# One-core encoder layer: transfers in another order, one more spinning matmul call, rows of x requested five steps ahead, the bias table built without TensorE, the last step by token halves

## The chip, the cores and the metric

The kernel runs on one core of a Trainium2 chip. The metric is the device time of one execution in microseconds. The engines are named as in the profile: PE multiplies matrices (PEld are its weight loads), DVE and ACT work on vectors, POOL does nothing of weight here, and SP only issues transfers (rows marked SPq).

## The reference, cut to what matters

```
xn = rms_norm(x, norm_g)                        # x: 256 tokens x 4096
h  = xn @ w_in                                  # 4096 x 14336
c_val, c_glu, c_gate, q, k, v, a_gate = split(h)
conv_out = silu(layer_norm(conv31(c_val * sigmoid(c_glu)))) * silu(c_gate)
attn_out = dilated_attention(rms(q), rms(k), v, rel_bias) * silu(a_gate)
y  = x + concat(conv_out, attn_out) @ w_out     # 4096 x 4096
```

All is float32. The relative bias is a table of 32 buckets by 16 heads, looked up by the bucket of the distance, plus the logarithm of how many of the three dilation patterns hold that distance.

## The kernel before, in words

The products are done in 18 groups of 1024 output columns: 14 groups of `w_in` columns (4 for the convolution, 8 for attention, 2 for the gate), then 4 of `w_out`. A group is 32 steps of 128 input channels; step n of the whole program (n from 0 to 575) handles channel block k = n mod 32. To keep float32 accuracy each operand is split in two parts in a shorter format: `wh` (ACT, L196) and `wl` (DVE, L197) of the weights, `xh` (ACT, L244) and `xl` (DVE, L245) of x. A step is 12 matmuls: for two column halves e and two token halves s, `xh*wh` (L621), `xl*wh` (L622) and `xh*wl` (L624).

Weights arrive as `raw` tiles, 1 MB each, one for two steps; three of them exist. The transfer of `raw(j+3)` is written right after the second split of `raw(j)` and waits for it. Splits are written three steps ahead of the products (`AHEAD = 3`). The transposed x arrives as `xT` tiles (four blocks each after the first few), and is split in the first group only and kept. In the same group the eight chunks of plain x (`x0` to `x7`, 512 KB each) are read to get the row norm: `load_x` requests a chunk, `square_x` (ACT, L237) squares it two and three steps later. From the sums `finish_rstd` makes `rstd`; as its yields are written out in the main loop, its root on ACT (L149) falls into step 29 and its end (L257) into step 30. The evacuation of the first group needs it at the end of step 31 (L575 on ACT for column half 0, L578 on DVE for half 1).

Nearly all transfers are issued by SP, strictly in program order: one whose wait is not met holds back all behind it. Every engine also takes its own instructions in program order. The bias table is made in `setup_gen`: a one-hot matrix times the table on PE (L281), a copy on ACT, and a store to `bias_dram`, from which attention reads it back much later. At the end of each `out` group, x is added to the accumulators (L563) and the result is stored (L565).

Of the kernel before, what the change touches and what calls it, by code (L numbers as in the profile page):

```python
# [11 lines left out]
F32 = mybir.dt.float32  # L12
# [20 lines left out]
DVE_STEP, ACT_STEP = 950, 1400  # L33
AHEAD = 3
RAW = 3
XN_LOAD = {2 + 3 * c: c for c in range(8)}
XN_SQUARE = {4 + 3 * c + s: (c, s) for c in range(8) for s in range(2)}
EVAC_TABLE = {"conv": AF.Sigmoid, "agv": AF.Silu, "gate": AF.Silu}
C_VAL, C_GLU, C_GATE, C_Q, C_K, C_V, C_AG = (2048 * i for i in range(7))

# [8 lines left out]
VECS = {"conv_b": 0, "ln_g": 16, "ln_b": 32, "q_g": 48, "k_g": 49}  # L49


def _bias_index():


    out = np.zeros((RB + 1, NDEL), np.float32)
    half, exact, dmax = RB // 2, RB // 4, 1024
    for m in range(NDEL):
        d = m - (S - 1)
        n = abs(d)
        if n < exact:  # L60
            b = n
        else:
            b = exact + int(
                np.float32(np.log(np.float32(n) / np.float32(exact)))
                / np.float32(math.log(dmax / exact))
                * np.float32(half - exact)
            )
            b = min(b, half - 1)
        b += half if d > 0 else 0
        out[b, m] = 1.0  # L70
        c = int(n <= 64) + int(n % 4 == 0 and n <= 256) + int(n % 16 == 0 and n <= 1024)
        out[RB, m] = math.log(c) if c else NEG
    return out


class Lane:
# [28 lines left out]
def layer_kernel(  # L105
# [4 lines left out]
    w,  # L110
    vecs,
    conv_w,
    rel_bias,
    bias_index,
    out,
):
    nc = tc.nc
# [9 lines left out]
    def t2(name):  # L127
        return sb.tile([P, 512], F32, tag="t2", bufs=6, name=name)
# [4 lines left out]
    def side(name):  # L133
        return ps.tile([P, 512], F32, tag="side", bufs=4, name=name)
# [36 lines left out]

    raw_tiles = {}

    def load_pair(j, cuts=(0, 2048)):

        g, jj = divmod(j, n_pairs)
        if g >= NG:
            return
        if groups[g][0] == "out":
            jj = (jj + n_pairs // 2) % n_pairs  # L180
        rt = sb.tile([P, 2048], F32, tag="raw", bufs=RAW, name=f"raw{j}")
        raw_tiles[j] = rt.rearrange("p (k c) -> p k c", k=2)
        for lo, hi in zip(cuts, cuts[1:]):
            nc.sync.dma_start(rt[:, lo:hi], w[g, jj, :, lo:hi])

    w_split = {}

# [76 lines left out]
    def setup_gen():  # L264
        for _ in range(8):
            yield
        nc.sync.dma_start(vec_cols, vecs)
        nc.sync.dma_start(wT.rearrange("p a b -> p (a b)"), conv_w)
        for _ in range(4):
            yield  # L270
        nc.vector.tensor_mul(gqk, col("q_g"), col("k_g"))
        yield
        rb = const.tile([RB + 1, NH], F32, name="rb")
        nc.gpsimd.memset(rb, 1.0)
        nc.sync.dma_start(rb[0:RB, :], rel_bias)
        oh = t2("oh")
        nc.sync.dma_start(oh[0 : RB + 1, :], bias_index)
        for _ in range(4):
            yield
        pb = side("pb")  # L280
        nc.tensor.matmul(pb[0:NH, :], rb, oh[0 : RB + 1, :], start=True, stop=True)  # L281
        yield
        tb = t2("tb")
        nc.scalar.copy(tb[0:NH, :], pb[0:NH, :])
        nc.sync.dma_start(bias_dram, tb[0:NH, :])
        yield

    aT, cT, mixA = {}, {}, {}
    conv_ready = {}
# [264 lines left out]

    xr_tiles = {}

    def evacuate(g, e, accs):
        kind, idx = groups[g][:2]
        rstd = state.get("rstd")
        if kind == "out":  # L560
            for s in range(2):
                t = xr_tiles[(g, e)][:, s, :]
                nc.vector.tensor_add(t, t, accs[s])  # L563
                c = groups[g][2 + e]
                nc.sync.dma_start(out[0][P * s : P * s + P, c : c + 512], t)  # L565
            return
        if kind == "conv" and e == 1:
            pair = state["sig"]
# [31 lines left out]

    accs = {}

    def products(n, e, part):

        g, k = divmod(n, KT)
# [24 lines left out]

    nc.scalar.dma_start(first_x, x_cols[:, 0 : KT + S])
    xT[0] = first_x[:, KT:]
    load_pair(0, (0, 512, 1024, 2048))
    load_xT(1, 1, nc.scalar)
    load_xT(2, 2, nc.scalar)
    load_pair(1, (0, 1024, 2048))
    load_xT(4, 4, nc.sync)
    load_pair(2)
    nc.scalar.copy(warm, ones[:, 0:1])
    spin = side("spin")  # L640
    for _ in range(6):
        nc.tensor.matmul(spin[:, :P], ones, ones, start=True, stop=True)

    split_w(0)
# [2 lines left out]
    for n in range(NG * KT):  # L647
# [19 lines left out]
        else:  # L667
# [8 lines left out]
            split_w(n + AHEAD)  # L676
            if k < KT - 1:
                products(n, 0, 1)
            else:
                products(n, 1, 0)  # L680
                products(n, 1, 1)
        if n % 4 == 0 and 8 + n < KT:
            load_xT(8 + n, 4, nc.sync)
        if n in XN_LOAD:
            load_x(XN_LOAD[n])
        if n in XN_SQUARE:
            square_x(*XN_SQUARE[n])
        if k == KT - 3 and groups[g][0] in EVAC_TABLE:
            nc.scalar.activation(warm, ones[:, 0:1], EVAC_TABLE[groups[g][0]])  # L689
        if 28 <= n <= 29:  # L690
            next(rstd_steps)
        elif n == 30:
            list(rstd_steps)
        pump()


_BIAS_INDEX = _bias_index()


def _layout(i):  # L700
# [4 lines left out]

    w_in, w_out = i["w_in"][0], i["w_out"][0]
    n_pairs = KT // 2
    w = np.empty((len(GROUPS), n_pairs, P, 2, 2, 512), np.float32)
    for g, (kind, _, *firsts) in enumerate(GROUPS):
        src = w_out if kind == "out" else w_in  # L710
# [8 lines left out]
        "w": w.reshape(len(GROUPS), n_pairs, P, 2048),  # L719
        "vecs": np.concatenate([cols(v) for v in vecs], axis=1),  # L720
        "conv_w": i["conv_w"][0].T.reshape(16, P, TAPS).transpose(1, 0, 2).reshape(P, -1),
        "rel_bias": i["rel_bias"],
        "bias_index": _BIAS_INDEX,
    }


# [27 lines left out]
```

## Time and profile before

| What | Value |
|---|---|
| Three runs | 1616.45, 1618.78 (median), 1620.45 us |
| Profiled execution, its own time | 1618.36 us |
| Its span in the profile | 1616.6 us |
| PE busy | 1605.7 us, 99% of the span, 7058 rows |
| DVE busy | 1072.2 us, 66% |
| ACT busy | 926.5 us, 57% |
| Moved by the core | 323.54 MB, mean 200 GB/s |

The profiled execution's own time is 1.76 us more than its span and 0.42 us below the median of the runs. Busy PE does not mean PE at its best: what a stretch costs is read from the starts of its matmuls.

### The profile page before, as it was taken

How to read it: one execution, taken by the hardware profiler on the slowest of the kernel's cores; microseconds unless marked ns; L12 is line 12 of the kernel's file. 1: busy time of each engine (PE TensorE's matmuls, PEld its weight loads, DVE VectorE, ACT ScalarE, POOL GpSimd, SP SyncE). 2: the span in 40 equal slices, each digit the busy share in tenths (PEclk: the TensorE clock that was granted, in tenths of full speed). 3: DMA queues.
4: the chain of work that ended last, by engine and by line, in shares of the span. 5: the costliest groups of instructions: out<-in, count | busy, mean ns of one | idle time of the engine just before them, and what ended most of it. 6: DMA issues, size and time to landing. Idle time of an engine off the chain costs nothing.

```text
span 1616.6 us, 18843 instructions
## 1 busy us (share of the span) xinstructions
PE 1605.7 (99%) x7058; PEld 1326.2 (82%) x7058; DVE 1072.2 (66%) x1440; ACT 926.5 (57%) x1415; POOL 0.3 (0%) x5
## 2 busy tenths in 40 slices
PE   8999999999999999999999999999999999999998
PEld 7878888888888888888888888888888888888887
DVE  5557888888888888678765555556466565454543
ACT  5664454545463456775778756774667973333332
POOL 0000000000000000000000000000000000000000
PEclk9999999999999999999999999999999999999999
DMA  8855555555555555555554555545555566566663
GB/s 308 326 182 189 202 185 190 199 197 194 190 201 185 202 186 194 191 180 186 205 185 176 200 188 192 192 176 197 201 194 179 194 210 228 212 222 220 214 229 104
DMA packets 52808, 323.54 MB, mean 200 GB/s; under 512 B 5819, under 2 KB 8251, under 8 KB 16108
## 3 DMA queue, kind: packets, MB, share of 16 engines
q1 hardware_dynamic: 52284, 321.79, 55.7%
q8 instruction: 55, 0.90, 0.2%
q10 hardware_dynamic: 432, 0.54, 0.1%
q14 instruction: 37, 0.30, 0.0%
HBM read 318.08 MB, written 4.23 MB: 199 GB/s over the span
## 4 chain that ended last, share of the span: by engine, by line
PE 96%; DMA 1%; ACT 1%; issue 0%; DVE 0%; SPq 0%; DVEq 0%; ACTq 0%
PE acc L621 32%; PE acc L622 31%; PE acc L624 31%; PE psc L475 1%; PE po L514 1%; DMA raw<-in_w_dram 1%; ACT wh L196 1%; DMA x<-in_x_dram 0%; ACT cT L400 0%; DMA first_x<-in_x_cols_dram 0%; DVE wl L197 0%; ACT qk L314 0%; ACT L689 0%; PE pb L281 0%; ACT conv L575 0%
## 5 line engine op out<-in xcount | busy, mean ns | idle before, releaser
L197 DVE TENSOR_TENSOR wl<-raw,wh 128x1024 fp32r<-128x1024 f32 x575 | 703.7, 1224 | 501.0 <-ACT wh L196 498.4
L196 ACT CAST wh<-raw 128x1024 fp32r<-128x1024 f32 x575 | 604.6, 1052 | 622.3 <-PE acc L622 433.4
L621 PE MATMUL acc<-wh,xh 128*128 128x512 f32 x1792 | 705.4, 394 | 5.2 <-ACT xh L244 1.8
L622 PE MATMUL acc<-wh,xl 128*128 128x512 f32 x1792 | 699.2, 390 | 0.0
L624 PE MATMUL acc<-wl,xh 128*128 128x512 f32 x1792 | 484.1, 389 | 0.0
L621 PEld LDWEIGHTS acc<-wh,xh 128*128 128x128 f32 x1792 | 337.4, 188 | 78.4 <-ACT conv L575 2.5
L622 PEld LDWEIGHTS acc<-wh,xl 128*128 128x128 f32 x1792 | 337.5, 188 | 70.2 <-DVE xl L245 0.2
L624 PEld LDWEIGHTS acc<-wl,xh 128*128 128x128 f32 x1792 | 336.3, 188 | 70.7 <-DVE wl L197 0.3
L346 DVE SCALAR_TENSOR_TENSOR cT<-conv,wT,cT 128x241 f32<-128x241 f32 (+14 forms) x480 | 201.6, 471 | 0.0
L621 PE MATMUL acc<-wh,mh 128*128 128x512 f32 x512 | 199.2, 389 | 0.0
L622 PE MATMUL acc<-wh,ml 128*128 128x512 f32 x512 | 199.2, 389 | 0.0
L624 PE MATMUL acc<-wl,mh 128*128 128x512 f32 x512 | 138.1, 389 | 0.0
L621 PEld LDWEIGHTS acc<-wh,mh 128*128 128x128 f32 x512 | 96.1, 188 | 20.0
L622 PEld LDWEIGHTS acc<-wh,ml 128*128 128x128 f32 x512 | 96.1, 188 | 20.0
L624 PEld LDWEIGHTS acc<-wl,mh 128*128 128x128 f32 x512 | 96.1, 188 | 19.9
L505 ACT COPY pr<-turn_p 32x128 f32<-32x128 f32 x256 | 75.9, 296 | 5.3 <-DVE turn_p L499 1.9
L245 DVE SCALAR_TENSOR_TENSOR xl<-xT,first_x,xh 128x256 fp32r<-128x256 f32 x31 | 14.9, 480 | 21.0 <-ACT xh L244 21.0
L314 ACT COPY qk<-turn_q 32x256 f32<-32x256 f32 x64 | 25.9, 404 | 1.2
L314 ACT COPY qk<-turn_k 32x256 f32<-32x256 f32 x64 | 25.8, 403 | 1.2 <-DVE turn_k L306 0.2
L314 ACT COPY agv<-turn_ag 32x256 f32<-32x256 f32 x64 | 25.8, 404 | 1.0
L314 ACT COPY conv<-turn_a 32x256 f32<-32x256 f32 x64 | 25.8, 403 | 1.1
L314 ACT COPY gate<-turn_g 32x256 f32<-32x256 f32 x64 | 25.9, 404 | 1.0
(126 smaller groups left out, 401.5 us busy)
## 6 DMA issues: line engine op xcount, KB each, us to landing
raw<-in_w_dram SPq DMA_DIRECT2D x286, 1024.0 KB, 4.8
x<-in_x_dram SPq DMA_DIRECT2D x8, 512.0 KB, 8.1
xr<-in_x_dram SPq DMA_DIRECT2D x8, 512.0 KB, 5.7
out_dram<-xr SPq DMA_DIRECT2D x16, 256.0 KB, 5.3
xT<-in_x_cols_dram SPq DMA_DIRECT2D x7, 512.0 KB, 7.7
T<-bias_dram SPq DMA_DIRECT2D x16, 192.0 KB, 4.9
raw<-in_w_dram SPq DMA_DIRECT2D x3, 512.0 KB, 8.9
raw<-in_w_dram SPq DMA_DIRECT2D x2, 256.0 KB, 5.2
```

The source lines that it names most:

```text
L196: nc.scalar.copy(wh, src)
L197: nc.vector.tensor_sub(wl, src, wh.bitcast(F32))
L245: nc.vector.scalar_tensor_tensor(l, src, g_cols[:, k : k + 1], h.bitcast(F32), op0=ALU.mult, op1=ALU.subtract)
L314: nc.scalar.copy(dst[32 * b : 32 * b + 32, :, :, to, :], backwards(v) if flip else v)
L346: nc.vector.scalar_tensor_tensor(c[:, t, lo:hi], a[:, t, lo + sh : hi + sh], wT[:, ch, k : k + 1], c[:, t, lo:hi], op0=ALU.mult, op1=ALU.add,)
L475: nc.tensor.matmul(psc[:, it, :], qt[hg][:, hh, P * it : P * it + P], kt[hg][:, hh, :], start=True, stop=True,)
L505: nc.scalar.copy(dst[32 * b : 32 * b + 32, :, :, 3 - a, :], backwards(blocks[32 * a : 32 * a + 32, :, :, b, :]),)
L514: nc.tensor.matmul(po[:, :S], vt[hg][:, jt, hs], pT[:, jt, :], start=jt == 0, stop=jt == 1)
L621: nc.tensor.matmul(a, hs, wp, start=k == 0, stop=False)
L622: nc.tensor.matmul(a, ls, wp, start=False, stop=False)
L624: nc.tensor.matmul(a, hs, wp, start=False, stop=k == KT - 1)
```

## The change

The first `xT` transfers move from ACT's queue to SP's, each between the pieces of `raw` beside which it is used, and `xT8` is requested before the loop. The spin loop has seven calls in place of six (each call shows as two PE rows, so 14 in place of 12). A chunk of x is requested five and six steps ahead of its two squares, in place of two and three, and the chunks follow every 2.5 steps, in place of 3. The steps of `finish_rstd` are written two to one step earlier: root in step 27, end in step 29. The bias table comes from two host-arranged rows per head that one DVE addition joins. In the last step of the program the three products of token half 0 all stand ahead of those of half 1, and half 1 is added and stored in two pieces of 256 columns, the first issued by ACT, the second by SP.

```diff
-XN_LOAD = {2 + 3 * c: c for c in range(8)}
-XN_SQUARE = {4 + 3 * c + s: (c, s) for c in range(8) for s in range(2)}
+XN_LOAD = {1 + (5 * c + 1) // 2: c for c in range(8)}
+XN_SQUARE = {n + 5 + s: (c, s) for n, c in XN_LOAD.items() for s in range(2)}
...
-    def load_pair(j, cuts=(0, 2048)):
+    def load_pair(j, cuts=(0, 2048), between=None):
...
             nc.sync.dma_start(rt[:, lo:hi], w[g, jj, :, lo:hi])
+            if between and hi == 1024:
+                between()
...
-        rb = const.tile([RB + 1, NH], F32, name="rb")
-        nc.gpsimd.memset(rb, 1.0)
-        nc.sync.dma_start(rb[0:RB, :], rel_bias)
-        oh = t2("oh")
-        nc.sync.dma_start(oh[0 : RB + 1, :], bias_index)
+        tb = t4("tb").rearrange("p a b -> p (a b)")[0:NH, :]
+        nc.sync.dma_start(tb, bias_rows)
         for _ in range(4):
             yield
-        pb = side("pb")
-        nc.tensor.matmul(pb[0:NH, :], rb, oh[0 : RB + 1, :], start=True, stop=True)
-        yield
-        tb = t2("tb")
-        nc.scalar.copy(tb[0:NH, :], pb[0:NH, :])
-        nc.sync.dma_start(bias_dram, tb[0:NH, :])
-        yield
+        nc.vector.tensor_add(tb[:, :NDEL], tb[:, :NDEL], tb[:, NDEL:])
+        nc.sync.dma_start(bias_dram, tb[:, :NDEL])
+        yield 600
...
+    def add_out(g, e, s, acc, queues=(nc.sync,)):
+        c, n = groups[g][2 + e], 512 // len(queues)
+        for i, queue in enumerate(queues):
+            t = xr_tiles[(g, e)][:, s, n * i : n * i + n]
+            nc.vector.tensor_add(t, t, acc[:, n * i : n * i + n])
+            queue.dma_start(out[0][P * s : P * s + P, c + n * i : c + n * i + n], t)
...
+    def last_products(n):
+        g, k = divmod(n, KT)
+        wh, wl = (t[:, 512:] for t in w_split[n])
+        for s in range(2):
+            a = accs[(g, 1)][s]
+            hs, ls = (t[:, P * s : P * s + P] for t in (mh[k], ml[k]))
+            nc.tensor.matmul(a, hs, wh, start=False, stop=False)
+            nc.tensor.matmul(a, ls, wh, start=False, stop=False)
+            nc.tensor.matmul(a, hs, wl, start=False, stop=True)
+            add_out(g, 1, s, a, (nc.scalar, nc.sync) if s else (nc.sync,))
...
-    load_pair(0, (0, 512, 1024, 2048))
-    load_xT(1, 1, nc.scalar)
-    load_xT(2, 2, nc.scalar)
+    load_pair(0, (0, 512, 1024, 2048), between=lambda: load_xT(1, 1, nc.sync))
+    load_xT(2, 2, nc.sync)
     load_pair(1, (0, 1024, 2048))
     load_xT(4, 4, nc.sync)
     load_pair(2)
+    load_xT(8, 4, nc.sync)
     nc.scalar.copy(warm, ones[:, 0:1])
     spin = side("spin")
-    for _ in range(6):
+    for _ in range(7):
         nc.tensor.matmul(spin[:, :P], ones, ones, start=True, stop=True)
...
-        if n % 4 == 0 and 8 + n < KT:
-            load_xT(8 + n, 4, nc.sync)
+        if n % 4 == 0 and 12 + n < KT:
+            load_xT(12 + n, 4, nc.sync)
...
-        if 28 <= n <= 29:
+        if 26 <= n <= 28:
             next(rstd_steps)
-        elif n == 30:
+        elif n == 29:
             list(rstd_steps)
```

Three places show how the order moves. The first is SP's queue from the start of the program, before (`raw0` to `raw5` are pairs of weight blocks, `xT8` the transposed x from block 8 on, `x0` a chunk of plain x):

```order
L184 DMA raw0_78<-in_w_dram 128x512 x2
L184 DMA raw0_78<-in_w_dram 128x1024
L184 DMA raw1_86<-in_w_dram 128x1024 x2
L223 DMA xT4_89<-in_x_cols_dram 128x1024
L184 DMA raw2_91<-in_w_dram 128x2048
L184 DMA raw3_119<-in_w_dram 128x2048
L184 DMA raw4_153<-in_w_dram 128x2048
L223 DMA xT8_155<-in_x_cols_dram 128x1024
L184 DMA raw5_189<-in_w_dram 128x2048
L232 DMA x0_193<-in_x_dram 128x2x512
```

The same queue of the changed kernel:

```order
L183 DMA raw0_78<-in_w_dram 128x512 x2
L224 DMA xT1_81<-in_x_cols_dram 128x256
L183 DMA raw0_78<-in_w_dram 128x1024
L224 DMA xT2_84<-in_x_cols_dram 128x512
L183 DMA raw1_86<-in_w_dram 128x1024 x2
L224 DMA xT4_89<-in_x_cols_dram 128x1024
L183 DMA raw2_91<-in_w_dram 128x2048
L224 DMA xT8_93<-in_x_cols_dram 128x1024
L183 DMA raw3_122<-in_w_dram 128x2048
L183 DMA raw4_156<-in_w_dram 128x2048
L224 DMA xT12_158<-in_x_cols_dram 128x1024
L233 DMA x0_174<-in_x_dram 128x2x512
```

`xT1` and `xT2` were ACT's and now stand inside and behind `raw0`; `xT8` has moved from behind `raw4` to ahead of `raw3`, and `x0` from behind `raw5` to ahead of it, with `xT12` before it. The second place is ACT at the end of the first group, before (`wh32` is the first weight block of the second group, `rxr` the root for `rstd`, `conv0_0` the evacuation):

```order
L196 CAST wh32_826<-raw16_718 128x1024
L689 ACT_TABLE_LOAD
L689 ACTIVATE warm_68<-ones_66 128x1
L149 ACT_TABLE_LOAD
L149 ACTIVATE rxr_813<-rxv_812 128x2
L196 CAST wh33_844<-raw16_718 128x1024
L575 ACT_TABLE_LOAD
L575 ACTIVATE conv0_0_865<-acc0_0_0_121,rstd_857 128x512
L575 ACTIVATE conv0_0_865<-acc0_0_1_122,rstd_857 128x512
```

ACT at the same place in the changed kernel:

```order
L197 CAST wh30_783<-raw15_669 128x1024
L148 ACT_TABLE_LOAD
L148 ACTIVATE rxr_766<-rxv_765 128x2
L245 ACTIVATE xh31_800<-xT28_529,first_x_69 128x256
L197 CAST wh31_804<-raw15_669 128x1024
L197 CAST wh32_824<-raw16_713 128x1024
L702 ACT_TABLE_LOAD
L702 ACTIVATE warm_68<-ones_66 128x1
L197 CAST wh33_846<-raw16_713 128x1024
L574 ACTIVATE conv0_0_860<-acc0_0_0_124,rstd_834 128x512
L574 ACTIVATE conv0_0_860<-acc0_0_1_125,rstd_834 128x512
```

The root now stands ahead of the table load for the evacuation, so that two table loads are left of three and none stands right ahead of `conv0_0`. The third place is the end of PE's program, before (`acc17_1_0` and `acc17_1_1` are the token halves of the last 512 columns):

```order
L621 MATMUL acc17_1_0_11574<-wh575_12040,mh31_10266 128x512
L622 MATMUL acc17_1_0_11574<-wh575_12040,ml31_10267 128x512
L621 MATMUL acc17_1_1_11575<-wh575_12040,mh31_10266 128x512
L622 MATMUL acc17_1_1_11575<-wh575_12040,ml31_10267 128x512
L624 MATMUL acc17_1_0_11574<-wl575_12041,mh31_10266 128x512
L624 MATMUL acc17_1_1_11575<-wl575_12041,mh31_10266 128x512
```

The same six products in the changed kernel:

```order
L609 MATMUL acc17_1_0_11569<-wh575_12035,mh31_10261 128x512
L610 MATMUL acc17_1_0_11569<-wh575_12035,ml31_10262 128x512
L611 MATMUL acc17_1_0_11569<-wl575_12036,mh31_10261 128x512
L609 MATMUL acc17_1_1_11570<-wh575_12035,mh31_10261 128x512
L610 MATMUL acc17_1_1_11570<-wh575_12035,ml31_10262 128x512
L611 MATMUL acc17_1_1_11570<-wl575_12036,mh31_10261 128x512
```

Token half 0 is finished three products before the end in place of one. From the second group to this last step nothing else is moved on any engine.

## Rows read from the trace of the kernel before

**Rows 1.** Busy time of each engine in stretches, then granted clock, DMA share, GB/s.

```profile
100.00:110.00 10.00, 9.86 (x36) 7.56 (x37) 6.86 (x8) 5.36 (x8) 0.00 (x0) 0.83 0.41 152
110.00:1590.00 1480.00, 1479.59 (x6529) 1225.12 (x6528) 999.90 (x1346) 852.80 (x1296) 0.00 (x0) 1.00 0.55 196
```

**Rows 2.** Timeline of PE: first products of steps 6 to 9 (start, duration).

```profile
23.04 0.39 PE L621 MATMUL acc<-wh,xh 128*128 128x512 f32 x1
...
25.76 0.39 PE L621 MATMUL acc<-wh,xh 128*128 128x512 f32 x1
...
30.18 0.50 PE L621 MATMUL acc<-wh,xh 128*128 128x512 f32 x1 [1.54 <-ACT wh L196]
...
33.06 0.39 PE L621 MATMUL acc<-wh,xh 128*128 128x512 f32 x1
```

**Rows 3.** Timeline of ACT, 20 to 31 us: the first square.

```profile
28.07 0.63 ACT L237 ACTIVATE junk<-x 128x512 f32<-128x512 f32 x1 [6.67 <-DMA x<-in_x_dram]
```

**Rows 4.** The chain of waits in order of time: start, duration, what.

```profile
5.61 10.03 DMA raw<-in_w_dram
...
19.99 8.06 DMA x<-in_x_dram
```

**Rows 5.** Timeline of PE around the bias matmul, steps 17 to 19.

```profile
54.82 0.39 PE L621 MATMUL acc<-wh,xh 128*128 128x512 f32 x1
...
57.63 1.03 PE L281 MATMUL pb<-oh,rb 33*16 33x512 f32 x2
...
61.46 0.39 PE L621 MATMUL acc<-wh,xh 128*128 128x512 f32 x1
```

**Rows 6.** Timeline of PE: first products of steps 31, 32 and 34.

```profile
94.10 0.39 PE L621 MATMUL acc<-wh,xh 128*128 128x512 f32 x1
...
100.14 0.50 PE L621 MATMUL acc<-wh,xh 128*128 128x512 f32 x1 [1.80 <-ACT conv L575]
...
106.13 0.39 PE L621 MATMUL acc<-wh,xh 128*128 128x512 f32 x1
```

**Rows 7.** Timeline of ACT at the end of the first group.

```profile
91.74 1.28 ACT L689 ACT_TABLE_LOAD   x1
...
93.26 1.28 ACT L149 ACT_TABLE_LOAD   x1
...
98.11 1.28 ACT L575 ACT_TABLE_LOAD   x1 [2.41 <-DVE rstd L257]
99.40 1.27 ACT L575 ACTIVATE conv<-acc,rstd 128x512 f32<-128x512 f32 x2
```

**Rows 8.** Timeline of DVE: the last two additions.

```profile
1612.18 1.29 DVE L563 TENSOR_TENSOR xr<-xr,acc 128x512 f32<-128x512 f32 x2 [1.43 <-PE acc L624]
```

**Rows 9.** Timeline of SP's queue: the last four stores.

```profile
1610.18 3.65 SPq L565 DMA_DIRECT2D out_dram<-xr  x4
```

**Rows 10.** Transfers of the last microseconds: count, size, median us to landing.

```profile
out_dram<-xr SPq DMA_DIRECT2D x4, 256.0 KB, 2.1
```

**Rows 11.** Timeline of PE: products of step 0, first product of step 2.

```profile
5.81 0.79 PE L621 MATMUL acc<-wh,xh 128*128 128x512 f32 x1 [1.82 <-ACT xh L244]
...
6.92 0.63 PE L621 MATMUL acc<-wh,xh 128*128 128x512 f32 x1
7.35 0.63 PE L622 MATMUL acc<-wh,xl 128*128 128x512 f32 x1
...
12.14 0.40 PE L621 MATMUL acc<-wh,xh 128*128 128x512 f32 x1
```

**Rows 12.** Timeline of ACT: the splits of weight blocks 2 and 6.

```profile
10.65 1.05 ACT L196 CAST wh<-raw 128x1024 fp32r<-128x1024 f32 x1
...
19.01 1.06 ACT L196 CAST wh<-raw 128x1024 fp32r<-128x1024 f32 x1 [0.44 <-DMA raw<-in_w_dram]
```

**Rows 13.** Timeline of SP's queue: the first five requests.

```profile
0.74 2.68 SPq L184 DMA_DIRECT2D raw<-in_w_dram  x5
```

**Rows 14.** Transfers issued around 2.1 us: the first half of `raw1`.

```profile
raw<-in_w_dram SPq DMA_DIRECT2D x1, 512.0 KB, 8.5
```

**Rows 15.** One stretch, columns as in the first group.

```profile
6.00:30.00 24.00, 22.56 (x90) 17.39 (x90) 13.04 (x18) 12.52 (x19) 0.00 (x0) 1.00 0.98 375
```

More of the change, by code (lines that the diff above doesn't have):

```diff
@@ L49, with _relative @@
 VECS = {"conv_b": 0, "ln_g": 16, "ln_b": 32, "q_g": 48, "k_g": 49}
-def _bias_index():
-    out = np.zeros((RB + 1, NDEL), np.float32)
+def _relative():
+    bucket, pattern = np.zeros(NDEL, np.int64), np.zeros(NDEL, np.float32)
     half, exact, dmax = RB // 2, RB // 4, 1024
@@ L69, in _bias_index @@
         b += half if d > 0 else 0
-        out[b, m] = 1.0
+        bucket[m] = b
         c = int(n <= 64) + int(n % 4 == 0 and n <= 256) + int(n % 16 == 0 and n <= 1024)
-        out[RB, m] = math.log(c) if c else NEG
-    return out
+        pattern[m] = math.log(c) if c else NEG
+    return bucket, pattern
 class Lane:
@@ L112, in layer_kernel @@
     conv_w,
-    rel_bias,
-    bias_index,
+    bias_rows,
     out,
@@ L561, in evacuate @@
             for s in range(2):
[L562 to L565, printed above, removed]
+                add_out(g, e, s, accs[s])
             return
@@ L678, in layer_kernel @@
                 products(n, 0, 1)
-            else:
+            elif n < NG * KT - 1:
                 products(n, 1, 0)
                 products(n, 1, 1)
-        if n % 4 == 0 and 8 + n < KT:
-            load_xT(8 + n, 4, nc.sync)
+            else:
+                last_products(n)
+        if n % 4 == 0 and 12 + n < KT:
+            load_xT(12 + n, 4, nc.sync)
         if n in XN_LOAD:
@@ L689, in layer_kernel @@
             nc.scalar.activation(warm, ones[:, 0:1], EVAC_TABLE[groups[g][0]])
-        if 28 <= n <= 29:
+        if 26 <= n <= 28:
             next(rstd_steps)
-        elif n == 30:
+        elif n == 29:
             list(rstd_steps)
         pump()
-_BIAS_INDEX = _bias_index()
 def _layout(i):
@@ L707, in _layout @@
     n_pairs = KT // 2
+    bucket, pattern = _relative()
     w = np.empty((len(GROUPS), n_pairs, P, 2, 2, 512), np.float32)
@@ L721, in _layout @@
         "conv_w": i["conv_w"][0].T.reshape(16, P, TAPS).transpose(1, 0, 2).reshape(P, -1),
-        "rel_bias": i["rel_bias"],
-        "bias_index": _BIAS_INDEX,
+        "bias_rows": np.concatenate(
+            [i["rel_bias"].T[:, bucket], np.tile(pattern, (NH, 1))], axis=1
+        ),
     }
```

## The prediction

> **What bounds the kernel now.** I read the busy times of stretches first, since PE is busy 99% of the span and only its losses can be won. From 110 to 1590 us PE is idle for 0.41 us of 1480 at a granted clock of 1.00, which is the 2.4 GHz level [rows 1]. All group boundaries but the first lie in it, and the change moves nothing between the second group and the last step, so it can win or lose only ahead of 110 us and behind 1590 us. Next I read PE's timeline for its pace: a full step is 12 products, and step 7 starts 25.76 − 23.04 = 2.72 us after step 6 [rows 2], or 0.2267 us a product. What PE's starts lag behind this pace is the loss of a place. There are five: the beginning, the first wait for x, the bias matmul, the first group's end, the tail. The chain of waits and the timelines of ACT, SP and DVE tell who is late there.
>
> **The wait for x: 1.86 us.** Step 9 should start at 25.76 + 2 × 2.72 = 31.20 and starts at 33.06 [rows 2]. ACT, in its own order, stood 6.67 us before the first square [rows 3], as `x0` was asked for at 19.99 and came 8.06 us later [rows 4]; behind that square stood the split of weight block 8, for which PE waited 1.54 us [rows 2]. Two steps of lead are 5.4 us, less than the 8.06; five are 13.6. But SP now asks for more ahead of `x0`. Behind `raw2`, which came at 5.61 + 10.03 = 15.64 [rows 4], stand `xT8`, `raw3`, `raw4`, `xT12` and `x0`, 3.67 MB; at the 375 GB/s that this stretch moved with its engines 0.98 busy [rows 15] that takes 9.8 us, so `x0` is there at 25.4. ACT comes to it after the splits of `raw4`, which lands at 15.64 + 2.62 MB / 375 GB/s = 22.6; two weight splits of 1.05 [rows 12] and one of x behind it are 25.2. ACT waits some 0.2 us, PE not at all. What is late next is `raw3`, since `xT8` (0.52 MB, 1.40 us at that rate) now goes ahead of it: the split of block 6 starts at 19.01 + 1.40 = 20.41 instead of 19.01 [rows 12] and ends at 21.46, while PE wants it at 23.04 less what the beginning wins. About 1.2 us of cover are left. I take the whole 1.86; the bounds are 0 (another wait of the same size takes its place) and 1.86.
>
> From then on a step asks for half a `raw` tile, a quarter of an `xT` tile, and 1/2.5 of a chunk: 0.524 + 0.131 + 0.210 = 0.865 MB in 2.72 us, 318 GB/s, where it was 0.830 MB or 305. Both lie under 375, so the queue runs ahead of PE.
>
> **The bias matmul: 1.20 us.** Step 19 should start 5.44 us after step 17's 54.82, and starts at 61.46 instead of 60.26 [rows 5]: two rows of PE for the small product, and a slow restart. All of it goes. In its place come one transfer of 64 KB, asked for four steps (10.9 us) ahead of its use, and one DVE addition of 16 x 512, for which the additions at the end, 0.64 us each [rows 8], are the nearest row. DVE's splits run steps ahead of PE; that lead is its cover. With the cover gone it would cost its 0.64, and a late table would hold DVE, with `wl` of the next block behind it, by as much as it is late. ACT loses a copy. I take 1.20, with 0.5 as the low bound.
>
> **The first group's end: 3.87 us.** From the first product of step 31 to that of step 34 lie 36 products (step 32 has only 6), or 8.16 us; the rows say 106.13 − 94.10 = 12.03 [rows 6]. PE waited 1.80 us for the evacuation, ran at a mean granted clock of 0.83 after it [rows 1], a mix of the levels of 1.2 and 2.4 GHz, and had been idle just before the clock fell. ACT tells why: it loads the table for the evacuation at 91.74, loads another for the root at 93.26, waits 2.41 us for `rstd` and then loads the first again, 1.28 us, at 98.11, ahead of 1.27 us of evacuation [rows 7]. The change puts the root in step 27, two steps ahead of where it was, and the end of `rstd` in step 29, so `rstd` comes some 5 us before it is asked for; the table load stays in step 29 and is not undone. Wait and reload leave the path, and the evacuation is then placed as at the other boundaries, where PE loses nothing that shows in the 0.41 us of the long stretch. Without the gap I expect the clock to stay at 2.4 GHz. I take 3.87; if only the reload goes, 1.28.
>
> **The beginning: 0.42 us.** PE's first product waits for the split of the first x, after 1.82 us of idleness [rows 11], which hides the two added spin rows. The products of step 0 start 0.43 us apart (6.92 and 7.35 [rows 11]), half of the pace. With `xT1` and `xT2` out of the way, the second quarter of `raw0` and its second half come sooner, and step 0 is done sooner whatever the clock does. But step 2 needs block 2, whose split ACT began at 10.65 and ended at 11.70 [rows 12] as `raw1` came; its bytes and those ahead of it are the same as before. So step 2 can start at 11.72 instead of 12.14 [rows 11]: 0.42. The low bound is 0, the high one 0.9: step 4's first product stands at 12.14 + 5.44 = 17.58, and the split of `raw2`, landed at 15.64, ends at 16.69.
>
> One rule speaks against this part. SP's five first requests took 2.68 us [rows 13], 0.54 each; two more put the request of `raw1` from 2.1 to about 3.2, and it landed 8.5 us after its request [rows 14], so 7.4 us of the way remain as cover. The Trainium skill (DMA: Bandwidth & Descriptors, section "Issuing engines are not separate DMA queues") says that all issuers share the same 16 engines, and that spreading requests only saves issue time. By that rule the move gives up two issue times, 1.07 us if they were on the path, which would turn the 0.42 into a loss of 0.65. The rows do not put them on it.
>
> **The tail: 0.70 us.** The last two additions start at 1612.18 and take 1.29 us for both [rows 8], so they end at 1613.47; SP has issued the last store at 1610.18 + 3.65 = 1613.83 [rows 9], and a store lands 2.1 us after its issue began [rows 10]. Now half 0 is added while PE does half 1's three products (0.68 us against 0.64). Behind the last product stand two additions of 256 columns: between 0.32 and 0.64 us each, I take 0.38, as the work is half. The last store is issued 0.53 us sooner and has half the bytes, 0.35 us less at 375 GB/s. Some of that is lost where three stores overlap: 0.70, between 0.2 and 0.9. The Trainium skill's rule named above would leave only the earlier issue, 0.53, for the tail, and a sum 0.17 lower.
>
> **Sum.** 1.86 + 1.20 + 3.87 + 0.42 + 0.70 = 8.05 us. Against the profiled execution's own 1618.36 this gives 1610.3; against the median of 1618.78, 1610.7. I forecast 1610.5, 0.5% faster. About 0.3%, 4.9 us, is what a measurement of this kernel can tell from no change, so faster means below 1613.9.
>
> **Rivals.**
> (a) The group's end stays late: ACT reaches the evacuation late for another reason, for instance because the table load and the last splits of x now meet. For it speaks that ACT holds a table load more in step 27, where x is still split; against it, that ACT loses one load of 1.28 in all. If all 3.87 stays, 1614.6: no change that can be told.
> (b) The wait for x only changes its name: block 6 or a later one waits for `raw3` behind `xT8`, or the beginning wins nothing. 1.86 and 0.42 stay: 1613.0. For it speaks the thin cover of 1.2 us, against it the 375 GB/s.
> (c) Slower: the transfers of steps 1 to 19 cannot keep up with 0.865 MB a step, PE runs at their pace, and every `raw` waits behind x in SP's order. This decides from 12.9 us of loss on, 8.05 won and 4.9 more, that is 0.68 us in each of 19 steps, or 254 GB/s. At 250 GB/s a step is 3.46 us, 14.1 us are lost: 1624.8. The row with 375 GB/s speaks against it.
> (d) The beginning gains its high bound, 0.9, because `raw1` comes sooner as well: 1610.0.
> (e) The change does less than its words: the spin does not raise the clock of step 0. This costs nothing of the sum, as block 2 bounds the step either way; it is part of the forecast.
>
> **Chances.** Forecast, with (e), 0.70 (own range 1609.0 to 1612.3), (a) 0.11, (b) 0.10, (d) 0.06, (c) 0.03. Faster takes forecast, (b) and (d): 0.86; within 0.3% is (a): 0.11; slower is (c): 0.03. For the range I leave out (a) and (c), and let the low end hold a tail and a beginning at their high bounds and the spread of runs: 1608.0 to 1614.0.
>
> **What would show it.** Right: no wait of PE for ACT between 12 and 110 us, and step 9 starting near 30.8; ACT's waits for x under 1 us each; no row of PE for the bias; two table loads near 75 to 90 us and none ahead of the evacuation; PE's starts 0.227 us apart over the boundary and a granted clock of 1.00 after it; the last store issued about 0.8 us behind the last product. Wrong: a PE wait for a split whose ACT row waits for `raw`; an evacuation that still waits for `rstd` or for ACT; the first product later than 5.81; a last store from ACT's queue that lands last.

## The result and the profile after

| | before | after |
|---|---|---|
| Median, four runs each | 1617.86 us | 1609.88 us |
| All runs | 1616.45 to 1620.45 | 1609.34 to 1610.65 |
| Profiled execution and its span | 1618.36, 1616.6 | 1610.65, 1608.9 |

The ratio after to before is 0.9949, with a 95% interval of 0.9932 to 0.9966: half a per cent faster, above the 0.3% that can be told apart here. The profiled executions differ by 7.71 us, the medians by 7.98.

Where these lie is read as in the prediction, from the starts of PE's products. The stretches of the profile after, with the columns of [rows 1]:

```profile
100.00:110.00 10.00, 10.00 (x46) 8.29 (x45) 4.74 (x5) 6.47 (x10) 0.00 (x0) 1.00 0.58 200
110.00:1590.00 1480.00, 1479.58 (x6529) 1225.18 (x6528) 999.90 (x1345) 850.92 (x1293) 0.00 (x0) 1.00 0.55 196
```

The long stretch is what it was; the 10 us behind the first boundary are now full and at a granted clock of 1.00 in place of 0.83. PE's timeline after, with the first products of steps 0, 1, 2, 9, 17, 19, 31 and 34, two more of step 0, and the last product:

```profile
5.41 0.80 PE L632 MATMUL acc<-wh,xh 128*128 128x512 f32 x1 [1.02 <-ACT xh L245]
...
8.23 0.63 PE L632 MATMUL acc<-wh,xh 128*128 128x512 f32 x1
8.66 0.63 PE L633 MATMUL acc<-wh,xl 128*128 128x512 f32 x1
...
10.39 0.39 PE L632 MATMUL acc<-wh,xh 128*128 128x512 f32 x1
...
11.76 0.39 PE L632 MATMUL acc<-wh,xh 128*128 128x512 f32 x1
...
30.80 0.39 PE L632 MATMUL acc<-wh,xh 128*128 128x512 f32 x1
...
52.55 0.39 PE L632 MATMUL acc<-wh,xh 128*128 128x512 f32 x1
...
57.99 0.39 PE L632 MATMUL acc<-wh,xh 128*128 128x512 f32 x1
...
90.64 0.39 PE L632 MATMUL acc<-wh,xh 128*128 128x512 f32 x1
...
98.79 0.39 PE L632 MATMUL acc<-wh,xh 128*128 128x512 f32 x1
...
1604.57 0.39 PE L611 MATMUL acc<-wl,mh 128*128 128x512 f32 x1
```

The last product of before is the second of the two in this row of its timeline, and starts at 1611.98:

```profile
1611.76 0.61 PE L624 MATMUL acc<-wl,mh 128*128 128x512 f32 x2
```

Set against the rows of before, each place gives its share:

| Place | Read from | Forecast | Measured |
|---|---|---|---|
| Beginning | step 2 at 12.14 [rows 11], now 11.76 | 0.42 | 0.38 |
| Wait for x | step 9 at 33.06 [rows 2], now 30.80: 2.26 ahead | 1.86 | 1.88 |
| Bias matmul | step 19 at 61.46 [rows 5], now 57.99: 3.47 ahead | 1.20 | 1.21 |
| First group's end | step 34 at 106.13 [rows 6], now 98.79: 7.34 ahead | 3.87 | 3.87 |
| Long stretch | lead of 7.34 at step 34, 7.42 at the last product | 0 | 0.08 |
| Tail | 4.6 us from the last product's start to the span's end, now 4.3 | 0.70 | 0.3 |

From step 17 to 19 are now 5.44 us and from step 31 to 34 8.15, which is 24 and 36 products at 0.2267.

ACT's timeline after, from the split of block 2 to the evacuation, shows why there is nothing left to wait for:

```profile
9.62 1.05 ACT L197 CAST wh<-raw 128x1024 fp32r<-128x1024 f32 x1 [0.46 <-DMA raw<-in_w_dram]
...
18.90 1.05 ACT L197 CAST wh<-raw 128x1024 fp32r<-128x1024 f32 x1 [1.38 <-DMA raw<-in_w_dram]
...
24.65 1.05 ACT L197 CAST wh<-raw 128x1024 fp32r<-128x1024 f32 x1 [1.25 <-PE acc L633]
25.60 0.63 ACT L238 ACTIVATE junk<-x 128x512 f32<-128x512 f32 x1
...
82.84 1.28 ACT L148 ACT_TABLE_LOAD   x1
88.32 1.28 ACT L702 ACT_TABLE_LOAD   x1
...
91.97 1.27 ACT L574 ACTIVATE conv<-acc,rstd 128x512 f32<-128x512 f32 x2 [0.94 <-PE acc L635]
```

The first square, at 25.60, waits for nothing (6.67 us in [rows 3]); just ahead of it ACT waits for PE, so ACT is now the one that is early. Two table loads are left here, the first of them for the root, and the evacuation waits 0.94 us for PE's own products, not for `rstd`.

### The profile page after: what moved, and what is told of

It is laid out like the page before. It is cut to its first block, busy times and chain, and to the rows that moved or that the text cites. A ratio compares the mean times of both kernels' runs of the same rounds, so it can differ in the third digit from the quotient of the medians.

```text
span 1608.9 us, 18840 instructions
## 1 busy us (share of the span) xinstructions
PE 1602.5 (100%) x7058; PEld 1326.6 (82%) x7058; DVE 1072.5 (67%) x1442; ACT 926.4 (58%) x1413; POOL 0.2 (0%) x4
## 4 chain that ended last, share of the span: by engine, by line
PE 98%; ACT 1%; DMA 0%; issue 0%; DVE 0%; DVEq 0%
PE acc L632 32%; PE acc L633 32%; PE acc L635 32%; PE psc L469 1%; PE po L508 1%; ACT cT L394 0%; ACT wh L197 0%; DMA first_x<-in_x_cols_dram 0%; ACT qk L308 0%; DVE wl L198 0%; DVE xr L556 0%; DVE qk L449 0%; ACT xh L245 0%; PE vapm L366 0%; PE mupm L366 0%
## 5 line engine op out<-in xcount | busy, mean ns | idle before, releaser
L483 ACT ACTIVATE pr<-pr,nm 128x256 f32<-128x256 f32 x32 | 16.0, 502 | 2.5 <-DVE nm L480 2.4
```

Source lines behind the costliest of these rows:

```text
L483: nc.scalar.activation(pi[:, it, :], pi[:, it, :], AF.Exp, bias=nm[:, it : it + 1], accum_out=z[:, it : it + 1],)
```

## Experiments

Each edit is made in the changed kernel, unless it is said otherwise, and each run had a profile. "Lost" and "won" are shifts of PE's starts against the profiled execution of the changed kernel.

**1. The lead of x back to two steps**

```diff
-XN_LOAD = {1 + (5 * c + 1) // 2: c for c in range(8)}
-XN_SQUARE = {n + 5 + s: (c, s) for n, c in XN_LOAD.items() for s in range(2)}
+XN_LOAD = {2 + 3 * c: c for c in range(8)}
+XN_SQUARE = {n + 2 + s: (c, s) for n, c in XN_LOAD.items() for s in range(2)}
```

> The changed kernel with one part undone: each chunk of x is requested two and three steps ahead of its squares, every 3 steps, as before; all else as changed. Theory (the short lead made the wait): ACT waits again some 4 to 6 us for x0, and PE waits for the split of block 8. With xT8 and xT12 now ahead of raw5 and x0 the request stands in another place than before, and by the landings of the changed kernel (raw5 at about 25.1 without x0 ahead, x0 at 26.4) block 8 is split at 28.7 where PE wants it at 28.1: a PE wait of 0.5 to 1.9 us at step 8, span 1609.4 to 1610.8. Rival (the other order of the first transfers removed the wait, not the lead): no wait of PE at step 8, span 1608.9.

Measured: 1611.93 us, span 1610.1. The waits of ACT for x are back, 6.22 us for the first square and 5.93 for a later one, and PE waits behind them. ACT's timeline, then PE's at steps 8 and 20:

```profile
26.73 0.63 ACT L238 ACTIVATE junk<-x 128x512 f32<-128x512 f32 x1 [6.22 <-DMA x<-in_x_dram]
```

```profile
28.85 0.50 PE L632 MATMUL acc<-wh,xh 128*128 128x512 f32 x1 [0.36 <-ACT wh L197]
...
61.87 0.50 PE L632 MATMUL acc<-wh,xh 128*128 128x512 f32 x1
```

PE loses 0.68 us at the first place and 0.36 at the second, with the slow products after each: 1.04 in all; 0.25 more are its beginning. The second loss was not expected. So the lead removes the wait. Taken back in the changed kernel it costs 1.04 and not 1.86. The other order of the transfers there (`xT8` stays ahead of `raw3`) is a likely reason, which no run tests.

**2. The five-step lead alone, in the kernel before** (the two lines that experiment 1's diff removes, put in place of its old ones, nothing else)

> The kernel before with one part of the change: the chunks of x are requested five and six steps ahead of their squares, every 2.5 steps; the first transfers, rstd, bias and tail as before. Theory (the short lead made the wait): PE's wait for block 8, 1.86 us with the restart, is gone, and no other appears; the beginning, the bias (1.2) and the first group's end (3.9) stay; span 1614.7 to 1615.0. Rival (without xT8 ahead of the loop the fuller queue makes block 8 or later ones late): PE still waits 0.5 us or more at steps 8 to 14.

Measured: 1617.47 us, span 1615.7. This execution began badly: step 5 stood 1.40 us behind that of before, with the products of step 0 0.43 us apart throughout. From there to step 9, at 32.60, its lag turns into a lead of 0.46, so the lead alone wins 1.86, exactly the term, and no other wait appears up to the first group's end. The span is longer than was expected, 1615.7 for 1615.0 at most, by the bad beginning.

PE still waits 1.80 us at the first group's end, but what follows is not what followed in before. PE's timeline, then the stretch with the columns of [rows 1]:

```profile
99.68 0.50 PE L621 MATMUL acc<-wh,xh 128*128 128x512 f32 x1 [1.80 <-ACT conv L575]
...
103.11 0.50 PE L621 MATMUL acc<-wh,xh 128*128 128x512 f32 x1 [0.75 <-DVE conv L578]
```

```profile
100.00:110.00 10.00, 9.25 (x39) 6.90 (x38) 7.37 (x8) 4.90 (x7) 0.00 (x0) 1.00 0.34 128
```

The clock stays at 2.4 GHz (granted 1.00, where [rows 1] have 0.83), and PE soon waits a second time, 0.75 us, for DVE's half of the evacuation. From step 31 to step 34 it loses 3.46 us, against 3.87 in before, where the products came more slowly and no second wait shows.

**3. The end of `rstd` late again**

```diff
-        if 26 <= n <= 28:
+        if 28 <= n <= 29:
             next(rstd_steps)
-        elif n == 29:
+        elif n == 30:
```

> The changed kernel with one part undone: the steps of rstd stand in steps 28 to 30 again. Theory (rstd came late): PE waits 1.8 us for the evacuation at the end of step 31, its products run at 1.2 GHz for some us after it, 36 products from step 31 to step 34 take 12.0 us instead of 8.2, span longer by 3.9 (1612.8). Rival (the first group's end was late because ACT and DMA lagged behind the waits for x, and they do no more): a loss under 1.3 us, span under 1610.2.

Measured: 1614.35 us, span 1612.6; 3.93 us are lost between steps 31 and 34. PE's timeline, then a stretch with the columns of [rows 1]:

```profile
96.39 0.50 PE L632 MATMUL acc<-wh,xh 128*128 128x512 f32 x1 [1.80 <-ACT conv L574]
...
98.95 0.63 PE L632 MATMUL acc<-wh,xh 128*128 128x512 f32 x1
99.38 0.63 PE L633 MATMUL acc<-wh,xl 128*128 128x512 f32 x1
```

```profile
98.00:101.00 3.00, 3.00 (x8) 1.94 (x8) 3.00 (x4) 0.79 (x1) 0.00 (x0) 0.50 0.00 0
```

The wait of 1.80 is the same as in [rows 6], and some products behind it they stand 0.43 apart until 101 us, at a granted clock of 0.50: PE stood idle, the clock fell to the lower of its levels, 1.2 GHz, and came back. Less than half of the loss is the wait itself. But the rest is not the price of the clock alone: in experiment 2 the clock did not fall behind the same wait, and only 0.4 to 0.5 us less were lost.

**4. The reload alone.** The early table load of the first group is left out, so that one load stands right ahead of the evacuation, with `rstd` in time.

```diff
-        if k == KT - 3 and groups[g][0] in EVAC_TABLE:
+        if k == KT - 3 and g and groups[g][0] in EVAC_TABLE:
```

> The changed kernel without the early table load in the first group (step 29), so that the table for the evacuation is loaded right ahead of it, with rstd long there. It tells apart the two parts of the loss at the first group's end. Theory (the lateness of rstd made the loss, the reload alone is covered): ACT has 0.9 us to spare ahead of the evacuation, so at most 0.4 of the 1.28 us shows there, and PE has 2.7 us of other products to do; no PE loss at the boundary, span 1608.9. Rival (the prediction's price for the reload alone): PE loses 1.28 us, span 1610.2.

Measured: 1609.22 us, span 1607.4. ACT's timeline:

```profile
89.59 1.28 ACT L574 ACT_TABLE_LOAD   x1
90.89 1.26 ACT L574 ACTIVATE conv<-acc,rstd 128x512 f32<-128x512 f32 x2
```

The load is on ACT ahead of the evacuation as before, and PE loses nothing: its lead over the changed kernel is 1.45 us ahead of the boundary and behind it. (The lead comes from the beginning, experiments 9 and 10.) With `rstd` in time the reload costs nothing; without the lateness there is no loss. A late `rstd` without a reload was not tried, so how the 3.87 would divide there stays open.

**5. The bias table on PE again** (the removed lines of the diff of `setup_gen` put back)

```diff
...
-        nc.vector.tensor_add(tb[:, :NDEL], tb[:, :NDEL], tb[:, NDEL:])
-        nc.sync.dma_start(bias_dram, tb[:, :NDEL])
-        yield 600
+        pb = side("pb")
+        nc.tensor.matmul(pb[0:NH, :], rb, oh[0 : RB + 1, :], start=True, stop=True)
...
```

> The changed kernel with the bias table made by PE again, all else as changed. Theory (the term of the sum): PE loses 1.2 us at the step where the two small rows stand, nothing elsewhere. Rival (the small product waited for its late operands, which the lighter queue brings sooner): 0.6 us or less.

Measured: 1610.96 us, span 1609.2. PE's timeline holds the two rows again:

```profile
54.24 1.03 PE L283 MATMUL pb<-oh,rb 33*16 33x512 f32 x2
```

From step 17 to step 19, between which the two rows stand, PE loses 1.20 us, the term. The span is only 0.3 longer, since this execution had won 1.13 in its beginning and lost 0.2 in its tail: a single time would have misled here, the starts do not.

**6. The last step's half 1 in one piece, by SP**

```diff
-            add_out(g, 1, s, a, (nc.scalar, nc.sync) if s else (nc.sync,))
+            add_out(g, 1, s, a)
```

> The changed kernel with one part undone: token half 1 of the last 512 columns is added in one piece and stored in one piece by SP; the token halves stay one after the other. The last store of the changed kernel was issued 1.20 us after the last product's start and landed 2.08 us later, as before with twice the bytes. Theory (landing does not depend on the bytes here, and two additions of 0.42 cost more than one of 0.69): the last store is issued 0.1 to 0.15 us sooner after the last product, the span is 0.1 shorter. Rival (the prediction's: half the bytes land 0.35 us sooner): the span is 0.2 to 0.35 us longer.

**7. The two pieces both by SP** (and ten spin calls, as in experiment 9)

```diff
-            add_out(g, 1, s, a, (nc.scalar, nc.sync) if s else (nc.sync,))
+            add_out(g, 1, s, a, (nc.sync, nc.sync) if s else (nc.sync,))
```

> The changed kernel with 10 spin calls and with both pieces of the last token half issued by SP, none by ACT. From the last product's start to the end of the span it was 4.29 us with the pieces on ACT and SP, and 4.03 with one whole piece on SP. Theory (the additions: two of 0.42 us in place of one of 0.69): 4.2 to 4.3 here. Rival (a store on ACT's queue lengthens the end): 4.03 to 4.15. It is also the fourth execution with 10 calls: if they bring the clock up early, PE's products run 0.227 us apart by the third product; if that is chance, this may fail here, as it did in four of eight executions with 7 calls.

Measured: 1610.02 us (span 1608.2) and 1609.6 (1607.8). From the start of the last product to the end of the span are 4.3 us in the changed kernel, 4.0 in experiment 6 and 4.3 in experiment 7. The additions of the changed kernel by shape (count, busy us, mean ns), in its last 7 us:

```profile
L556 DVE TENSOR_TENSOR xr<-xr,acc 128x512 f32<-128x512 f32 x3 | 2.0, 686 | 6.1 <-PE acc L635 5.2 <-PE acc L611 1.0
...
L556 DVE TENSOR_TENSOR xr<-xr,acc 128x256 f32<-128x256 f32 x2 | 0.8, 418 | 0.0
```

Its stores there (count, size, median us to landing):

```profile
out_dram<-xr SPq DMA_DIRECT2D x3, 256.0 KB, 2.1
out_dram<-xr ACTq DMA_DIRECT2D x1, 128.0 KB, 2.1
out_dram<-xr SPq DMA_DIRECT2D x1, 128.0 KB, 2.1
```

And those of experiment 6:

```profile
out_dram<-xr SPq DMA_DIRECT2D x4, 256.0 KB, 2.0
```

Two halves take 0.84 us of DVE against 0.69 for the whole, and a store of half the size lands no sooner. So the pieces win nothing and cost 0.3; which queue issues the first is of no weight. The theory of experiment 6 had only 0.1: the two additions overlap, so the last store of the whole piece is issued 1.14 us behind the start of the last product, 0.07 sooner than with pieces. It also lands 0.07 sooner after its issue, and the other half of the 0.3 lies behind the landing, where no run tells its cause. Against before, experiment 6 has 4.0 for 4.6, with the order of the last products as the one difference in its tail: what won there is only that half 0 is finished three products before the end.

**8. `xT1` and `xT2` on ACT's queue again**

```diff
-    load_pair(0, (0, 512, 1024, 2048), between=lambda: load_xT(1, 1, nc.sync))
-    load_xT(2, 2, nc.sync)
+    load_pair(0, (0, 512, 1024, 2048))
+    load_xT(1, 1, nc.scalar)
+    load_xT(2, 2, nc.scalar)
```

> The changed kernel with one part undone: xT1 and xT2 are requested by ACT again, all else as changed. In the changed kernel and four versions of it the first half of raw1 landed at 9.0 to 9.6 us and raw2 at 14.1 to 14.6; before, at 10.6 and 15.6. Theory (two queues that ask for small rows at once make the first megabytes slower): raw1's half lands at 10.3 to 10.7 again, raw2 at 15.2 to 15.7, PE's first product stands at 5.7 to 5.8. Rival (executions differ by as much in their first transfers): landings as in the changed kernel.

Measured: 1611.47 us, span 1609.7; step 5 starts at 20.74, against 19.91. The first transfers of the changed kernel, issued in its first 10 us:

```profile
raw<-in_w_dram SPq DMA_DIRECT2D x3, 512.0 KB, 6.5
...
raw<-in_w_dram SPq DMA_DIRECT2D x2, 256.0 KB, 4.2
```

And those of this experiment:

```profile
raw<-in_w_dram SPq DMA_DIRECT2D x3, 512.0 KB, 8.2
...
raw<-in_w_dram SPq DMA_DIRECT2D x2, 256.0 KB, 5.0
```

The same bytes, asked for by SP alone, come sooner where they are wanted first: the second quarter of `raw0` lands at 5.64 in the changed kernel and at 6.95 here (7.37 before), the first half of `raw1` at 9.59 and at 10.27 (10.63 before). In nine other executions with the changed order (all experiments but 2, 8 and 12) they land at 5.46 to 5.69 and 9.03 to 9.55, so this is no scatter. PE's timeline of the experiment:

```profile
6.57 0.39 PE L632 MATMUL acc<-wh,xh 128*128 128x512 f32 x1
6.80 0.40 PE L633 MATMUL acc<-wh,xl 128*128 128x512 f32 x1
7.64 0.51 PE L632 MATMUL acc<-wh,xh 128*128 128x512 f32 x1 [0.45 <-ACT wh L203]
...
8.38 0.63 PE L632 MATMUL acc<-wh,xh 128*128 128x512 f32 x1
8.80 0.63 PE L633 MATMUL acc<-wh,xl 128*128 128x512 f32 x1
```

PE was already at 2.4 GHz (products 0.23 apart) when it had to wait 0.45 us for that quarter; behind the wait they stand 0.42 apart, and from 8 to 11 us the granted clock is 0.50. PE had also been idle for 1.30 us ahead of its first product, so the wait need not be the only cause. The 0.83 us at step 5 is less firm than the landings, since the clock alone moves that step by more (experiments 9 and 10). Nothing was gained in exchange: `xT1` and `xT2` land later too, at 7.13 and 9.29 us, against 6.06 and 8.30.

**9. Ten spin calls in place of seven**

```diff
-    for _ in range(7):
+    for _ in range(10):
         nc.tensor.matmul(spin[:, :P], ones, ones, start=True, stop=True)
```

> The changed kernel with 10 spin calls (20 rows of PE) in place of 7, so that PE is busy right up to its first product. In five executions with 7 calls PE was idle about 1.0 us ahead of the first product, and the products came to the pace of 2.4 GHz at quite different times, from the third product of step 0 on (step 1 starting at 8.6 us) to the end of step 0 (10.6). Theory (what PE did ahead of the first product decides when the clock rises): the clock is at 2.4 GHz by the second or third product, step 1 starts at 8.6 or sooner. Rival (the moment is a matter of chance, whatever PE does): step 1 starts anywhere from 8.6 to 10.6. First product at 5.4 to 5.5 either way.

Measured: 1609.34 us, span 1607.5. PE's timeline, with the spin, the third and fourth product and step 1:

```profile
1.05 4.33 PE L653 MATMUL spin<-ones 128*128 128x128 f32 x20 [1.05 <-DVE ones L136]
...
6.31 0.39 PE L632 MATMUL acc<-wh,xh 128*128 128x512 f32 x1
6.53 0.39 PE L633 MATMUL acc<-wh,xl 128*128 128x512 f32 x1
...
8.60 0.39 PE L632 MATMUL acc<-wh,xh 128*128 128x512 f32 x1
```

The spin ends 0.07 us ahead of the first product, at 5.45, instead of 1.02. PE is at 2.4 GHz with its third product, step 1 starts 1.79 us sooner and step 5, at 18.60, 1.31.

**10. The changed kernel once more**, five runs, on the same chip as experiments 11 and 12

> The changed kernel itself once more, beside the two versions with 10 spin calls on the same chip. Median 1609.9, span 1607.4 to 1609.0 by where the clock rises: step 1 anywhere from 8.6 to 10.6 us by the theory that 7 calls leave it to chance; if it starts at 8.6 here as well, the 10 calls are not shown to do anything.

Measured: median 1610.24 us (1609.54 to 1610.96), ratio 0.9949 with an interval of 0.9937 to 0.9962: the same verdict. But PE's timeline of this execution differs in its beginning, at steps 1 and 2:

```profile
8.54 0.50 PE L632 MATMUL acc<-wh,xh 128*128 128x512 f32 x1
...
10.67 0.50 PE L632 MATMUL acc<-wh,xh 128*128 128x512 f32 x1
```

The same program reached 2.4 GHz with its third product here, and between its eighth and the end of step 0 in the first profile. (From 6 to 9 us the profile prints a granted clock of 1.00 for both, so the level is read from the pace there: 0.43 us apart is the pace that goes with the 0.50 of experiment 3.) So experiment 9 alone does not show that ten calls raise the clock. Of eight executions with seven calls four were early (experiments 4, 5, 8 and 10), of four with ten calls all four. That fits, and could be chance. One thing more speaks for the calls. With seven, the early executions have a first product of 0.49 to 0.51 us, and those that start with one of 0.79 or 0.80 keep the slow pace up to their eighth. With ten, two executions (experiments 7 and 12) start with a slow product of 0.79 and 0.76 us, and the pace has risen by the third or fourth. PE's timeline of experiment 7:

```profile
5.53 0.79 PE L632 MATMUL acc<-wh,xh 128*128 128x512 f32 x1
...
6.45 0.39 PE L632 MATMUL acc<-wh,xh 128*128 128x512 f32 x1
```

No execution with seven calls shows a rise at this place. These are still only four executions.

**11. Ten calls and the whole last piece** (the edits of experiments 6 and 9), five runs

> A version meant to beat both: the changed kernel with 10 spin calls and with token half 1 of the last columns added and stored in one piece. Theory (10 calls keep PE busy up to its first product and bring 2.4 GHz there each time; the whole store ends sooner): first product at 5.4 to 5.5, step 1 at 8.6, 4.0 us from the last product's start to the end of the span in place of 4.3; 0.3 us at the tail and, as 7 calls reached the early clock in only some executions, 0.5 to 1.2 at the beginning: span 1606.9 to 1607.6, median 1608.5 to 1609.2. Rival (the clock rises by chance): step 1 between 8.6 and 10.6, span 1607.2 to 1608.7.

Measured: median 1609.51 us (1609.17 to 1610.08), ratio to before 0.9944, 0.9930 to 0.9957; 0.73 us below experiment 10, of which the profile shows 0.3 in the tail. The ranges of runs overlap, so this is the best version, by a margin at the edge of what can be told. Only the tail came as the theory said: the first product stands at 5.73, step 1 at 8.90, the span is 1607.9 and the median lies above the range of 1608.5 to 1609.2; step 1 and the span lie in the rival's ranges. Yet the rival's reason is not what made it late: from the first product to step 1 are 3.17 us, as in experiment 9 (3.15); it is `first_x` that landed late, at 5.14 against 4.86 there.

**12. All first transfers on one queue**: experiment 11 with `first_x` requested by SP, ahead of `raw0`

```diff
-    nc.scalar.dma_start(first_x, x_cols[:, 0 : KT + S])
+    nc.sync.dma_start(first_x, x_cols[:, 0 : KT + S])
```

> The version with 10 spin calls and the whole last store, and the very first transfer (first_x) also asked for by SP, ahead of raw0, so that one queue carries all first transfers. Theory (two queues asking at once slow the first rows): first_x lands sooner than 4.9 us, PE's first product stands ahead of 5.4, though raw0 is asked for one issue time (0.43 us) later. Rival (the first landings are set by the issue and by the start of the engines): raw0's first quarter lands 0.3 to 0.5 us later, the first product at 5.7 to 5.9. Step 1 about 3.2 us behind the first product by the clock's theory; that is the third execution with 10 calls.

Measured: 1610.54 us, span 1608.7, step 5 at 20.02. Transfers of its first 10 us:

```profile
raw<-in_w_dram SPq DMA_DIRECT2D x3, 512.0 KB, 7.1
...
first_x<-in_x_cols_dram SPq DMA_DIRECT2D x1, 144.0 KB, 2.2
```

`first_x` lands 2.2 us after its request, at 2.94, where it took 4.1 beside SP's queue. But the quarters of `raw0` land at 4.75 and 6.58, the first half of `raw1` at 10.60, and PE waits 0.26 and 0.38 us for their splits. The first product stands at 5.35, as the theory said, but nothing is gained: what follows comes later, up to step 5 by 0.81 us against experiment 11. So one queue for all is not enough for early landings: the first half of `raw1` is as late here as in before, and 1.28 us later than in experiment 11, where its request stood only 0.47 sooner.

## Why the prediction was right

1609.88 lies in the range and in the forecast's own range, 0.6 below the 1610.5 forecast; the kernel before, too, came out 0.9 lower in its median than the 1618.78 that the forecast started from. By parts:

**Wait for x, bias matmul, first group's end: right in size,** within 0.02 us each, and in mechanism but for one part of the last; each alone or undone answers by itself (experiments 1 to 3, 5). Rival (a), a late boundary, and (b), the renamed wait, did not come about: ACT's waits for `raw3`, `raw4` and x ended ahead of PE's need, `x0` landing at 23.92 against the 25.4 estimated; nor did (c), the queue that cannot keep up. That the clock stays up behind the boundary without the gap came true (granted 1.00). But the fall of the clock was worth little of the 3.87: experiment 2 lost 3.46 at this place without it, by a second wait for DVE's half of the evacuation, which the prediction did not see. The price given for half of it, "if only the reload goes, 1.28", has no run for it, and experiment 4 speaks against pricing it by the reload's duration, since there a reload that stands ahead of an evacuation whose operand is there cost nothing.

**The beginning: right size by luck, wrong bound.** The step that failed is "its bytes and those ahead of it are the same as before", from which block 2's split was to start at 10.65 as before. It starts at 9.62 and ends at 10.67, while step 2 starts at 11.76: it was not the bound in the profile of the result. That was step 0 at 1.2 GHz, 4.98 us up to step 1 against 4.78 before (step 1 at 10.59 there, in the timeline of [rows 11]); the first product came 0.40 sooner, and from step 1 to step 2 it took 1.37 in place of 1.55. In experiment 10, where the clock rose early, the split of block 2 is the bound again (step 2 at 10.67), and step 2 stands 1.47 ahead of before; by step 5, behind `raw2`, 0.92 of it are left, the gain of rival (d). Over the seven executions with the changed beginning and seven calls, step 5 stands 0.15 to 1.86 us ahead of before, and the two with the old beginning (before and experiment 2) are 1.40 apart. So that one pair of executions gave 0.38 where 0.42 was forecast is chance. That (e), a spin that does nothing, would cost nothing of the sum was wrong as well: the clock of step 0 moves the end by up to some 1.4 us (the lead of 1.45 in experiment 4).

Putting the two requests back on ACT's queue (experiment 8) brings `raw0`'s second quarter 1.31 us later, and early requests on that queue are what differs. It lands within 0.2 us of `xT1` there, at 6.95 and 7.13. The Trainium skill (DMA: Bandwidth & Descriptors, section "Issuing engines are not separate DMA queues") says that transfers of different issuers interleave on the same engines, and with that the runs agree. It also says that more issuers only save issue time, by which the term would have been a loss of 0.65: that price the runs don't bear out. Why the early landings are slower with those requests on ACT's queue stays open. That they took their share from the weights cannot be all of it, as the x tiles came later too, and with everything on one queue (experiment 12) the landings were late as well.

**The tail: right mechanism, half the size,** 0.3 for 0.70. Two sub-terms were mis-sized. The last store is issued 1.20 us behind the start of the last product, where it was 1.52: 0.32 sooner, not 0.53, and not the 0.8 behind that product which was to be a sign of being right. I set 1.29 us of additions against 0.76, but the 1.29 began at 1612.18 [rows 8], 0.19 ahead of the end of PE's last row (1611.76 and 0.61 long in the timeline of before), while the two pieces now begin behind it. And the 0.35 for a store of half the size is 0, with 2.1 us to landing for 256 KB and for 128 KB. The halves even cost 0.3 against one whole piece (experiment 6).

**Sum:** 7.7 us where 8.05 was forecast. The tail is 0.4 short, and the long stretch gave 0.08, which was not forecast.

**Open.** Whether three more spin calls settle the clock of step 0, or only met four early executions. What slows the first landings in experiments 8 and 12. Why `raw2` lands anywhere between 14.1 and 15.3 us in executions with the same requests. And what makes up the time between the last landing and the end of the span, 1.00 us in the changed kernel and 0.86 in experiment 6.

## What to carry to other kernels

A wait of PE can cost more than its length: 1.80 us of waiting for a late `rstd` cost 3.46 to 3.93 in three executions, with the clock down in two of them and with a second wait in the third. So look for the late operand even where an engine looks busy with something else ahead of it, such as a table load. Look where early requests stand that are wanted later: on a second queue they came with later landings of what was wanted first, though one queue for everything was no better. Splitting the last piece of work pays only if the transfer's time depends on its size there; at 128 to 256 KB it did not.

## What the runs showed of the hardware

The same program, run again, had TensorE at 2.4 GHz from its third product in one execution and only by the end of step 0 in another, 1.09 us apart at step 2 (11.76 and 10.67) and 0.51 at step 5 (19.91 and 19.40). A wait of 0.45 us soon after the rise was followed by a return to 1.2 GHz (experiment 8, where PE had also been idle for 1.30 us ahead of its first product), while the waits of 0.26 and 0.38 in experiment 12, whose spin had run up to the first product, were not. And the same wait of 1.80 us at the same place was followed by a granted clock of 0.50 in experiment 3, and by one of 1.00 over the next 10 us in experiment 2. Stores of 256 and 128 KB at the end of the program landed 2.0 to 2.1 us after their issue alike.
